# Reordering the seven block products of a channel mixer, and making their normed operand one tile earlier

## The chip, the cores and the metric

The kernel runs on one core of a Trainium2 chip. The metric is the device time of one execution in microseconds (us), as the median of several runs; less is better. All times of single instructions come from one profiled execution.

## The reference

A trunk of two layers over 512 frames of width 1024. Layer 0 mixes time with an RWKV-7 recurrence, layer 1 with chunked attention; both add attention into 256 memory tokens and an output projection. Each layer ends with the channel mixer that the change touches, a gated unit with a convolution over time:

```python
def conv_glu(h, w_in, conv_w, conv_b, w_out):
    seq = h.shape[1]
    gate, val = jnp.split(h @ w_in, 2, axis=-1)
    gp = jnp.pad(gate, ((0, 0), (CONV_W - 1, 0), (0, 0)))
    conv = conv_b + sum(conv_w[j] * gp[:, j:j + seq] for j in range(CONV_W))
    return (jax.nn.gelu(conv, approximate=False) * val) @ w_out
...
        x = x + conv_glu(rms_norm(x, ln2[layer]), ffn_in[layer], ffn_conv[layer],
                         ffn_conv_b[layer], ffn_out[layer])
```

D_FF is 2816, which is 22 tiles of 128 hidden columns; `w_in` makes a gate and a value for each.

## The kernel before

Activations lie transposed: 128 features on the partitions, 512 frames along a row. Every float32 operand is split into a high part and a low remainder, and a product is three passes of TensorE: high weight by high input, high weight by low input (these two alternate), then low weight by high input. The high part is made by ScalarE (`whi`, L169), the remainder by VectorE (`wlo`, L175). The split weights live in rings of three buffers each, the raw weights of the tiles below in a ring of two (`raw`).

A channel mixer (`ffn`) goes over the 22 hidden tiles in order, in two ways:

- `plain(j)`: tiles 0 to 5, 9, 13, 17, 20 and 21. Gate and value are 24 matmuls of 512 columns each (L198, L199, L202). Tiles 0 to 5 read the input before normalisation and multiply by `rho` afterwards (L390, L393).
- `seven(j)`: the other eleven tiles. Gate and value, each 2 by 2 blocks of inputs and frames, are made from seven block products instead of eight, Strassen-like. Each product (`prod`) is 12 matmuls of 256 columns: 8 with the high weights (L403), 4 with the low (L405). VectorE adds the weights up first (L415, L416, L419), and combines the results (L427, L429, L431, L433, L437).

The results lie in four PSUM tiles of 512 columns, one bank each, `f1` to `f4`; the ring `F` (name `psf`) has four banks. `h1` and `h2` are the halves of a bank. The products read pieces of the normed input (`XN`, tiles N) and four combinations of it (`XT`, tiles M). The framework that places the waits treats a bank as one thing: a product that starts a new sum in a bank waits until what was read from that bank, in either half, has been read.

The normed input and its combinations are made by `normed(k4)`, in four parts, each beside one plain tile. It uses a buffer of the ring `raw`, so the first weights for `seven` can be loaded only when these buffers come free.

The queues of the engines are filled by a list scheduler of the framework, which keeps to the order of the code unless it expects an engine to wait. So the order on an engine can differ from the order of the code; it is fixed when the program is built.

In layer 0 the matmul inputs of the seven products are called `r2h`/`r2l` (N) and `r1h`/`r1l` (M), in layer 1 `nh`/`nl` and `r2h`/`r2l`.

Of the kernel before, what the change touches and what calls it, by code (L numbers as in the profile page):

```python
# [13 lines left out]
ALU = mybir.AluOpType  # L14
# [5 lines left out]
S = 512  # L20
# [91 lines left out]
def trunk_kernel(ctx, tc, A, out):  # L112
    nc = tc.nc
    PE, V, SC, GP = nc.tensor, nc.vector, nc.scalar, nc.gpsimd
# [23 lines left out]
    def Vc(name, i):  # L138
        return vec[:, VOFF[name][0] + i:VOFF[name][0] + i + 1]
# [20 lines left out]
    def tmp(dt=F32, shape=(P, S)):  # L160
        return banks["tmp"].tile(list(shape), dt, name="tmp", tag="tmp")
# [180 lines left out]
    T1, T3, T2, T4 = range(4)  # L342

    def normed(k4, l, hp, xT, Nh, Nl, Mh, Ml):

        x2 = [tmp() for _ in range(2)]
        for u in range(2):
            k = k4 + 4 * u
            V.scalar_tensor_tensor(x2[u][:], xT[:, k], Vc(f"ln2_{l}", k), rho[:], op0=ALU.mult, op1=ALU.mult)
            split_to(Nh[:, k], Nl[:, k], x2[u][:])  # L350
        q = lambda i: x2[i // 2][:, i % 2 * 256:i % 2 * 256 + 256]
        su = hp.tile([P, 7, S], F32, name="raw", tag="raw", bufs=2)[:].rearrange("p a s -> p (a s)")[:, 0:1024]
        s_ = [su[:, i * 256:(i + 1) * 256] for i in range(4)]
        V.tensor_tensor(s_[T1], q(1), q(0), op=ALU.subtract)
        V.tensor_tensor(s_[T3], q(1), q(3), op=ALU.subtract)
        V.tensor_tensor(s_[T2], q(3), s_[T1], op=ALU.subtract)
        V.tensor_tensor(s_[T4], q(2), s_[T2], op=ALU.subtract)
        split_to(*(t[:, 2 * k4:2 * k4 + 2].rearrange("p a s -> p (a s)") for t in (Mh, Ml)), su)

    def ffn(l, hp, U, M, N, new_u, xT, after, last=None):  # L360


        (Uh, Ul), (Mh, Ml), (Nh, Nl) = U, M, N
        sp = hp.tile([P, 7, S], F32, name="sp", tag="sp")
        hid32 = {j: sp[:, j] for j in range(6)}

        def conv(g, j):
            c = tmp()
            SC.activation(c[:], g, AF.Identity, scale=Vc(f"cw2_{l}", j), bias=Vc(f"cb_{l}", j))
            conv_rest(c, g, j)  # L370
            return c

        def conv_rest(c, g, j):
            V.scalar_tensor_tensor(c[:, 1:S], g[:, 0:S - 1], Vc(f"cw1_{l}", j), c[:, 1:S], op0=ALU.mult, op1=ALU.add)
            V.scalar_tensor_tensor(c[:, 2:S], g[:, 0:S - 2], Vc(f"cw0_{l}", j), c[:, 2:S], op0=ALU.mult, op1=ALU.add)
            SC.activation(c[:], c[:], AF.Gelu)

        def plain(j, act, normed_):
            wg = load_w(A["ffn_in"][l, j, 0])
            wv = load_w(A["ffn_in"][l, j, 1])  # L380
            pg = ps_f()
            run(dense(pg[:], [(wg, K8)], act))
            pv = ps_f()
            run(dense(pv[:], [(wv, K8)], act))
            if normed_:
                c = conv(pg[:], j)
                V.tensor_tensor(hid32[j], pv[:], c[:], op=ALU.mult)
                return
            g = tmp()
            V.tensor_tensor(g[:], pg[:], rho[:], op=ALU.mult)  # L390
            c = conv(g[:], j)
            v = tmp()
            V.tensor_tensor(v[:], pv[:], rho[:], op=ALU.mult)  # L393
            V.tensor_tensor(hid32[j], v[:], c[:], op=ALU.mult)

        XN = lambda k0, h: [tuple(t[:, k0 + k, h * 256:h * 256 + 256] for t in (Nh, Nl)) for k in range(4)]
        XT = lambda i: [tuple(t[:, 2 * k + i // 2, i % 2 * 256:i % 2 * 256 + 256] for t in (Mh, Ml)) for k in range(4)]

        def prod(ps, w, x):
            (wh, wl), o = w  # L400
            for k in range(4):
                for n in range(2):
                    PE.matmul(ps, wh[:, o + k * P:o + k * P + P], x[k][n], start=k == n == 0, stop=False)  # L403
            for k in range(4):
                PE.matmul(ps, wl[:, o + k * P:o + k * P + P], x[k][0], start=False, stop=k == 3)  # L405

        def seven(j):

            raw = hp.tile([P, 7, S], F32, name="raw", tag="raw", bufs=2)
            g_, v_ = A["ffn_in"][l, j, 0], A["ffn_in"][l, j, 1]  # L410
            G1, S2, V2, G2, S3, S1, V1 = range(7)
            S4 = V1
            for o, src in ((V1, v_[:, 0:S]), (G1, g_[:, 0:S]), (V2, v_[:, S:2 * S]), (G2, g_[:, S:2 * S])):
                nc.sync.dma_start(raw[:, o], src)
            V.tensor_tensor(raw[:, S3:S1 + 1], raw[:, G1:V2 + 1:2], raw[:, V1:V1 + 1].to_broadcast([P, 2, S]), op=ALU.add)  # L415
            V.tensor_tensor(raw[:, S2], raw[:, S1], raw[:, G1], op=ALU.add)  # L416
            two = lambda o: split_w(raw[:, o:o + 2].rearrange("p a s -> p (a s)"), 1024)
            w_g1s2, w_s3s1, w_v2g2 = two(G1), two(S3), two(V2)
            V.tensor_tensor(raw[:, S4], raw[:, S2], raw[:, G2], op=ALU.add)  # L419
            w_s4 = split_w(raw[:, S4], S)  # L420
            h1, h2 = slice(0, 256), slice(256, 512)
            f1, f2, f3, f4 = (ps_f() for _ in range(4))
            g, c, v = tmp(), tmp(), tmp()
            prod(f1[:, h1], (w_g1s2, 0), XN(0, 0))
            SC.copy(g[:, h1], f1[:, h1])
            prod(f1[:, h2], (w_g1s2, S), XT(T2))
            V.tensor_tensor(g[:, h2], g[:, h1], f1[:, h2], op=ALU.subtract)  # L427
            prod(f2[:, h1], (w_s3s1, 0), XT(T3))
            V.tensor_tensor(c[:, h1], f2[:, h1], g[:, h2], op=ALU.subtract)  # L429
            prod(f3[:, h2], (w_s3s1, S), XT(T1))  # L430
            V.tensor_tensor(g[:, h2], g[:, h2], f3[:, h2], op=ALU.subtract)  # L431
            prod(f3[:, h1], (w_v2g2, 0), XT(T4))
            V.tensor_tensor(v[:].rearrange("p (a s) -> p a s", a=2), c[:, h1].unsqueeze(1).to_broadcast([P, 2, 256]),  # L433
                            f3[:].rearrange("p (a s) -> p a s", a=2), op=ALU.add)
            prod(f4[:, h1], (w_v2g2, S), XN(4, 0))
            prod(f4[:, h2], (w_s4, 0), XN(4, 1))
            V.tensor_tensor(g[:], g[:], f4[:], op=ALU.add)  # L437
            SC.activation(c[:], g[:], AF.Identity, scale=Vc(f"cw2_{l}", j), bias=Vc(f"cb_{l}", j))
            conv_rest(c, g[:], j)
            V.tensor_tensor(hid32[j], v[:], c[:], op=ALU.mult)  # L440

        hid = {}

        def halves(j, h, lo):
            hid[j] = h, lo
            split_to(h, lo, hid32[j])

        for j in range(PLAIN_RAW):
            plain(j, pair_of(Uh, Ul), False)
            if 1 <= j <= 4:  # L450
                normed(j - 1, l, hp, xT, Nh, Nl, Mh, Ml)
        u32 = [new_u(i, F32) for i in range(2)]
        for j in range(6, NFF):
            hid32[j] = u32[(j - 6) // 8][:, (j - 6) % 8]
        for j in range(PLAIN_RAW, NFF):
            if j in BY_SEVEN:
                seven(j)
            else:
                plain(j, pair_of(Nh, Nl), True)
            if j == NFF - 2:  # L460
                hl = [hp.tile([P, 7, S], F32R, name="hl", tag="raw", bufs=2) for _ in range(2)]
                for k in range(8, 15):
                    halves(k, hl[0][:, k - 8], hl[1][:, k - 8])
        for k in range(8):
            halves(k, Mh[:, k], Ml[:, k])
        uh = new_u(0, F32R)
        sl = hp.tile([P, 7, S], F32R, name="sl", tag="sp")
        for k in range(15, NFF):
            halves(k, uh[:, k - 15], sl[:, k - 15])
        for m in range(KD):  # L470
            us = []
            for lo, n in ((8, 7), (0, 8), (15, 7)):
                us.append((load_w(A["ffn_out"][l, m][:, lo * P:(lo + n) * P], n * P), list(range(lo, lo + n))))
            if m == KD - 1 and last is not None:
                last(us, lambda k: hid[k])
                break
            ps = ps_d()
            run(dense(ps[:], us, lambda k: hid[k]))
            V.tensor_tensor(xT[:, m], xT[:, m], ps[:], op=ALU.add)  # L479
            after(m)  # L480
# [612 lines left out]
    xT = mid.tile([P, KD, S], F32, name="xT")  # L1093
# [8 lines left out]
    hp = fctx.enter_context(tc.tile_pool(name="hpA", bufs=1))  # L1102
# [201 lines left out]
    with ExitStack() as fctx:  # L1304
        open_banks(fctx, S=2, F=4)
        open_tmp(fctx, 6)
        hp = fctx.enter_context(tc.tile_pool(name="hpB", bufs=1))
# [125 lines left out]
```

## Time and profile before

| | |
|---|---|
| median of 3 runs | 1368.42 us (1364.19 to 1369.57) |
| the profiled execution's own time | 1365.64 us |
| its span, first to last instruction | 1363.8 us |
| TensorE busy | 97% |
| VectorE busy | 68% |
| ScalarE busy | 49% |
| mean granted TensorE clock | 0.989 |

The profiled execution was 2.78 us faster than the median of the runs, so a sum made on it is carried to the median by that offset. A span is what one execution's records cover; the execution's own time adds 1.84 us around it.

### The profile page before, as it was taken

Reading aid. Unit: us, or ns where it says so; the run is one execution under the profiler, and the core shown is the slowest. Engines: PE = TensorE matmul, PEld = TensorE weight load, DVE = VectorE, ACT = ScalarE, POOL = GpSimd, SP = SyncE. Lnnn points to the kernel's source line nnn. Section 1 sums busy time; section 2 is a strip of 40 time slices with the busy share of each in tenths; the row PEclk is TensorE's granted clock in tenths of the full one; section 3 lists DMA queues with packets and bytes.
Section 4 is the critical chain, followed back from the end, with each engine's and each line's share of the span. In section 5 each row is a group of like instructions: output and inputs, shape, how many; then the busy total and the mean of one; then the engine's idle time right before and its main releaser. Section 6 shows DMA issues by size and latency. Waiting matters only on the chain. (4 is left out here: it accounts for less than half of the span.)

```text
span 1363.8 us, 24368 instructions
## 1 busy us (share of the span) xinstructions
PE 1318.7 (97%) x9826; PEld 1104.1 (81%) x9826; DVE 926.9 (68%) x1806; ACT 674.5 (49%) x1142; POOL 34.2 (3%) x57
## 2 busy tenths in 40 slices
PE   6999999999999999999999999999999999999996
PEld 5786777777788899998888778786788999888886
DVE  7865677664667998889333666747669988893324
ACT  6556566554544444455222576657444544472221
POOL 3000000000000000000000000000000000000000
PEclk9998999998999999999999999999999999999998
DMA  5376544551132332313323422222323332223322
GB/s 181 86 179 148 114 93 98 114 135 38 65 116 84 124 124 66 120 64 89 99 85 101 144 86 86 93 91 89 94 87 123 107 100 94 93 74 97 100 88 75
DMA packets 87904, 137.76 MB, mean 101 GB/s; under 512 B 44144, under 2 KB 47856, under 8 KB 87792
## 3 DMA queue, kind: packets, MB, share of 16 engines
q1 hardware_dynamic: 85056, 126.25, 30.9%
q0 software_dynamic: 2736, 9.96, 4.2%
q8 instruction: 77, 1.26, 0.4%
q14 instruction: 35, 0.29, 0.1%
HBM read 129.37 MB, written 6.82 MB: 100 GB/s over the span
## 5 line engine op out<-in xcount | busy, mean ns | idle before, releaser
L175 DVE TENSOR_TENSOR wlo<-wraw,whi 128x1024 fp32r<-128x1024 f32 (+1 forms) x139 | 165.3, 1191 | 140.7 <-PE psd L202 130.9
L169 ACT CAST whi<-wraw 128x1024 fp32r<-128x1024 f32 (+1 forms) x158 | 162.0, 1027 | 195.4 <-DMA wraw<-in_ffn_out_dram 50.1
L198 PE MATMUL psd<-r1h,whi 128*128 128x512 f32 (+1 forms) x399 | 161.0, 405 | 1.1 <-ACT whi L169 1.0
L199 PE MATMUL psd<-r1l,whi 128*128 128x512 f32 x336 | 132.9, 396 | 0.0
L169 ACT CAST whi<-raw 128x1024 fp32r<-128x1024 f32 x88 | 81.8, 940 | 85.2 <-PE psf L403 55.9
L202 PE MATMUL psd<-r1h,wlo 128*128 128x512 f32 (+1 forms) x399 | 107.0, 397 | 0.0
L175 DVE TENSOR_TENSOR wlo<-raw,whi 128x1024 fp32r<-128x1024 f32 x88 | 95.3, 1086 | 5.4 <-ACT whi L169 5.3
L198 PEld LDWEIGHTS psd<-r1h,whi 128*128 128x128 f32 x399 | 75.8, 190 | 20.6 <-issue 3.0
L202 PEld LDWEIGHTS psd<-r1h,wlo 128*128 128x128 f32 x399 | 72.9, 191 | 14.2 <-issue 0.3
L403 PE MATMUL psf<-r2h,whi 128*128 128x256 f32 x308 | 79.4, 288 | 1.8 <-ACT whi L169 1.3
L403 PE MATMUL psf<-r2l,whi 128*128 128x256 f32 x308 | 77.6, 283 | 0.0
L198 PE MATMUL psd<-r2h,whi 128*128 128x512 f32 (+1 forms) x200 | 77.4, 391 | 0.1
L199 PE MATMUL psd<-r2l,whi 128*128 128x512 f32 (+1 forms) x200 | 76.2, 384 | 0.8 <-DVE r2l L215 0.8
L199 PEld LDWEIGHTS psd<-r1l,whi 128*128 128x128 f32 x336 | 63.9, 190 | 11.1
L231 ACT ACTIVATE tmp<-xT 128x512 f32<-128x512 f32 x27 | 17.0, 631 | 103.4 <-DVE xT L479 88.4
L403 PEld LDWEIGHTS psf<-r2h,whi 128*128 128x128 f32 x308 | 58.8, 191 | 5.2 <-ACT whi L169 1.7
L403 PEld LDWEIGHTS psf<-r2l,whi 128*128 128x128 f32 x308 | 58.9, 191 | 0.2
L202 PE MATMUL psd<-r2h,wlo 128*128 128x512 f32 (+1 forms) x200 | 50.9, 386 | 0.0
L405 PE MATMUL psf<-r2h,wlo 128*128 128x256 f32 x308 | 49.4, 283 | 0.4 <-DVE wlo L175 0.4
L403 PE MATMUL psf<-r1h,whi 128*128 128x256 f32 x176 | 46.3, 294 | 0.4 <-DVE tmp L431 0.4
L198 PE MATMUL psd<-hl,whi 128*128 128x512 f32 (+1 forms) x119 | 44.4, 377 | 0.0
L199 PE MATMUL psd<-sl,whi 128*128 128x512 f32 (+1 forms) x119 | 44.4, 377 | 0.0
(450 smaller groups left out, 3270.9 us busy)
## 6 DMA issues: line engine op xcount, KB each, us to landing
wraw<-in_ffn_in_dram SPq DMA_DIRECT2D x44, 512.0 KB, 3.8
raw<-in_ffn_in_dram SPq DMA_DIRECT2D x88, 256.0 KB, 3.7
wraw<-in_ffn_out_dram SPq DMA_DIRECT2D x32, 448.0 KB, 3.4
wraw<-in_wA_dram SPq DMA_DIRECT2D x20, 512.0 KB, 4.2
wlo<-in_wA_dram POOLq DMA_DIRECT2D x17, 512.0 KB, 7.2
wraw<-in_w_out_dram SPq DMA_DIRECT2D x16, 512.0 KB, 3.8
wraw<-in_ffn_out_dram SPq DMA_DIRECT2D x16, 512.0 KB, 3.5
wraw<-in_wB_dram SPq DMA_DIRECT2D x8, 512.0 KB, 3.6
```

Of the source, the lines that this page charges most:

```text
L169: SC.copy(hi[:, :n], raw)
L175: V.tensor_tensor(lo[:, :n], raw, hi[:, :n], op=ALU.subtract)
L198: PE.matmul(ps, wh[:, j * P:(j + 1) * P], ah, start=start and n == 0, stop=False)
L199: PE.matmul(ps, wh[:, j * P:(j + 1) * P], al, start=False, stop=False)
L202: PE.matmul(ps, wl[:, j * P:(j + 1) * P], act(k)[0], start=False, stop=stop and n == len(ks) - 1)
L231: SC.activation(sq[:], src, AF.Square)
L403: PE.matmul(ps, wh[:, o + k * P:o + k * P + P], x[k][n], start=k == n == 0, stop=False)
L405: PE.matmul(ps, wl[:, o + k * P:o + k * P + P], x[k][0], start=False, stop=k == 3)
```

## The change

Two edits in `ffn`, for both layers. In `seven`, the second product goes into a new bank (`f2`) and not into the other half of the bank that ScalarE reads at that moment; the third goes back to the first bank; and the fifth is issued directly after the fourth, into the other half of the same bank, ahead of the VectorE instruction that reads the fourth's result. In the loop over tiles 0 to 5, `normed` is called beside tiles 0 to 3 and not 1 to 4. The arithmetic is the same, and no instruction is added or removed.

```diff
             prod(f1[:, h1], (w_g1s2, 0), XN(0, 0))
             SC.copy(g[:, h1], f1[:, h1])
-            prod(f1[:, h2], (w_g1s2, S), XT(T2))
-            V.tensor_tensor(g[:, h2], g[:, h1], f1[:, h2], op=ALU.subtract)
-            prod(f2[:, h1], (w_s3s1, 0), XT(T3))
-            V.tensor_tensor(c[:, h1], f2[:, h1], g[:, h2], op=ALU.subtract)
+            prod(f2[:, h1], (w_g1s2, S), XT(T2))
+            V.tensor_tensor(g[:, h2], g[:, h1], f2[:, h1], op=ALU.subtract)
+            prod(f1[:, h2], (w_s3s1, 0), XT(T3))
+            V.tensor_tensor(c[:, h1], f1[:, h2], g[:, h2], op=ALU.subtract)
+
             prod(f3[:, h2], (w_s3s1, S), XT(T1))
+            prod(f3[:, h1], (w_v2g2, 0), XT(T4))
             V.tensor_tensor(g[:, h2], g[:, h2], f3[:, h2], op=ALU.subtract)
-            prod(f3[:, h1], (w_v2g2, 0), XT(T4))
...
         for j in range(PLAIN_RAW):
             plain(j, pair_of(Uh, Ul), False)
-            if 1 <= j <= 4:
-                normed(j - 1, l, hp, xT, Nh, Nl, Mh, Ml)
+            if j < 4:
+                normed(j, l, hp, xT, Nh, Nl, Mh, Ml)
```

The lines after the reordered products stand one lower in the changed file: L431 is L433 there, and L433 is L434.

What becomes of it on the engines, at three places. First TensorE, tile 10 of layer 0 (the tile whose span the prediction follows matmul by matmul). `psf_6158` to `psf_6161` are its banks `f1` to `f4`; `whi_6141` holds the weights of the first pair of products, `whi_6145` of the second. Before, from the end of the first product to the start of the second in `f1`:

```order
L405 MATMUL psf_6158<-r2h_4908,wlo_6142 128x256 x4
L403 MATMUL psf_6159<-r1h_68,whi_6145 128x256
L403 MATMUL psf_6159<-r1l_69,whi_6145 128x256
...
L403 MATMUL psf_6158<-r1h_68,whi_6141 128x256
L403 MATMUL psf_6158<-r1l_69,whi_6141 128x256
```

and now:

```order
L405 MATMUL psf_6158<-r2h_4908,wlo_6142 128x256 x4
L403 MATMUL psf_6159<-r1h_68,whi_6141 128x256
L403 MATMUL psf_6159<-r1l_69,whi_6141 128x256
...
L405 MATMUL psf_6159<-r1h_68,wlo_6142 128x256 x4
L403 MATMUL psf_6158<-r1h_68,whi_6145 128x256
L403 MATMUL psf_6158<-r1l_69,whi_6145 128x256
```

Before, the scheduler put four matmuls of the product into `f2` between the first product and the second in `f1`; now the whole product into `f2`, twelve matmuls, stands there, and no product is cut in two any more. The same holds at `f3`: before, five matmuls of the sixth product stood between the fourth and the fifth; now the fifth follows the fourth with nothing between them.

Second VectorE in the same tile. `wlo_6155` is the last weight remainder of this tile, `wlo_6268` and `wlo_6272` are the first of the next. Before:

```order
L427 TENSOR_TENSOR tmp_6162<-tmp_6162,psf_6158 128x256
L175 TENSOR_TENSOR wlo_6155<-raw_6134,whi_6154 128x512
L429 TENSOR_TENSOR tmp_6163<-psf_6159,tmp_6162 128x256
L431 TENSOR_TENSOR tmp_6162<-tmp_6162,psf_6160 128x256
L175 TENSOR_TENSOR wlo_6268<-raw_6260,whi_6267 128x1024
L433 TENSOR_TENSOR tmp_6164<-tmp_6163,psf_6160 128x512
L415 TENSOR_TENSOR raw_6386<-raw_6386 128x1024
L175 TENSOR_TENSOR wlo_6272<-raw_6260,whi_6271 128x1024
```

and now:

```order
L427 TENSOR_TENSOR tmp_6162<-tmp_6162,psf_6159 128x256
L175 TENSOR_TENSOR wlo_6155<-raw_6134,whi_6154 128x512
L429 TENSOR_TENSOR tmp_6163<-psf_6158,tmp_6162 128x256
L175 TENSOR_TENSOR wlo_6268<-raw_6260,whi_6267 128x1024
L433 TENSOR_TENSOR tmp_6162<-tmp_6162,psf_6160 128x256
L434 TENSOR_TENSOR tmp_6164<-tmp_6163,psf_6160 128x512
L415 TENSOR_TENSOR raw_6386<-raw_6386 128x1024
L175 TENSOR_TENSOR wlo_6272<-raw_6260,whi_6271 128x1024
```

The subtraction from the fourth product's result (L431, now L433) went behind a weight remainder of the next tile, and waits for two products in place of one; L415, which waits for a load of raw weights, still stands ahead of the next tile's second remainder.

Third VectorE in layer 0 at the change from plain tiles to `seven`. `raw_5688` belongs to tile 6, the first of that kind, `psf_5626` and `psf_5651` are the gate and value of plain tile 5. Before:

```order
L357 TENSOR_TENSOR raw_5607<-tmp_5600,raw_5607 128x256
L390 TENSOR_TENSOR tmp_5676<-psf_5626,rho_71 128x512
L215 TENSOR_TENSOR r1l_69<-raw_5607,r1h_68 128x1024
L374 SCALAR_TENSOR_TENSOR tmp_5678<-tmp_5676,vec_67,tmp_5678 128x511
L415 TENSOR_TENSOR raw_5688<-raw_5688 128x1024
L375 SCALAR_TENSOR_TENSOR tmp_5678<-tmp_5676,vec_67,tmp_5678 128x510
L416 TENSOR_TENSOR raw_5688<-raw_5688 128x512
L419 TENSOR_TENSOR raw_5688<-raw_5688 128x512
L393 TENSOR_TENSOR tmp_5683<-psf_5651,rho_71 128x512
L175 TENSOR_TENSOR wlo_5696<-raw_5688,whi_5695 128x1024
```

and now (`psf_5579` is the value of plain tile 4):

```order
L415 TENSOR_TENSOR raw_5688<-raw_5688 128x1024
L375 SCALAR_TENSOR_TENSOR tmp_5606<-tmp_5604,vec_67,tmp_5606 128x510
L393 TENSOR_TENSOR tmp_5611<-psf_5579,rho_71 128x512
L416 TENSOR_TENSOR raw_5688<-raw_5688 128x512
L394 TENSOR_TENSOR sp_5193<-tmp_5611,tmp_5606 128x512
L419 TENSOR_TENSOR raw_5688<-raw_5688 128x512
L175 TENSOR_TENSOR wlo_5696<-raw_5688,whi_5695 128x1024
L415 TENSOR_TENSOR raw_5814<-raw_5814 128x1024
L390 TENSOR_TENSOR tmp_5676<-psf_5626,rho_71 128x512
```

Tile 6's weights are added up ahead of the gate of plain tile 5, and not after it. On the load queue (SP), tile 6's four raw loads (L414) stand one place earlier, ahead of the two loads for plain tile 9. From plain tile 20 on, each engine's order is as before, and nothing moves outside the two mixers.

## The prediction

> **What bounds the kernel now.** I read the page first: the busy line and the chain that ended last.
>
> ```profile
> PE 1318.7 (97%) x9826; PEld 1104.1 (81%) x9826; DVE 926.9 (68%) x1806; ACT 674.5 (49%) x1142; POOL 34.2 (3%) x57
> PE 33%; DVE 4%; ACT 2%; issue 1%; DMA 0%; DVEq 0%; SPq 0%; ACTq 0%
> ```
>
> TensorE carries the span; what the change can win is time in which TensorE stands still. The busy time does not show all of it, because the records of waiting matmuls overlap. So I looked at the stretches of the change: plain tiles 0 to 5 of layer 0, then from the first block product to plain tile 20 in each layer (busy time in us per engine, then granted clock).
>
> ```profile
> 411.00:471.50 60.50, 60.50 (x270) 49.87 (x268) 51.02 (x76) 27.54 (x34) 0.00 (x0) 1.00 0.33 106
> 472.97:621.86 148.89, 148.06 (x1068) 138.79 (x1069) 128.87 (x178) 75.50 (x101) 0.00 (x0) 1.00 0.28 87
> 1059.08:1207.23 148.15, 147.38 (x1068) 138.69 (x1069) 129.07 (x179) 75.48 (x101) 0.00 (x0) 1.00 0.27 87
> ```
>
> The clock is full there, and VectorE is busy 128.87 of 148.89 us. The timeline of TensorE then gives the pace without stops: an undisturbed product, the two halves of a plain tile, and the ends of the stretches.
>
> ```profile
> 520.14 0.28 PE L403 MATMUL psf<-r1h,whi 128*128 128x256 f32 x1
> 521.58 0.28 PE L403 MATMUL psf<-r2h,whi 128*128 128x256 f32 x1
> ...
> 627.33 0.39 PE L198 MATMUL psf<-r2h,whi 128*128 128x512 f32 x1
> 632.77 0.39 PE L198 MATMUL psf<-r2h,whi 128*128 128x512 f32 x1
> ```
>
> A product is 1.44 us (12 steps of 0.12), seven are 10.08. Half a plain tile is 5.44 (24 steps of 0.2267), a tile 10.88. The stretch holds eleven tiles of the one kind and three of the other: 11 × 10.08 + 3 × 10.88 = 143.52 us. It takes 148.89 and 148.15, so stops cost 5.37 in layer 0 and 4.63 in layer 1.
>
> Where they stand, in tile 10:
>
> ```profile
> 517.02 0.28 PE L403 MATMUL psf<-r1h,whi 128*128 128x256 f32 x1
> ...
> 517.38 0.28 PE L403 MATMUL psf<-r1l,whi 128*128 128x256 f32 x1
> 517.65 0.38 PE L403 MATMUL psf<-r1h,whi 128*128 128x256 f32 x1
> 517.87 0.28 PE L403 MATMUL psf<-r1l,whi 128*128 128x256 f32 x1
> ...
> 522.06 0.28 PE L403 MATMUL psf<-r2h,whi 128*128 128x256 f32 x1
> 522.25 0.39 PE L403 MATMUL psf<-r1h,whi 128*128 128x256 f32 x1
> 522.48 0.28 PE L403 MATMUL psf<-r1l,whi 128*128 128x256 f32 x1
> ```
>
> ```profile
> 517.22 0.37 ACT L425 COPY tmp<-psf 128x256 f32<-128x256 f32 x1 [1.55 <-PE psf L405]
> 521.78 0.42 DVE L431 TENSOR_TENSOR tmp<-tmp,psf 128x256 f32<-128x256 f32 x1 [0.97 <-PE psf L405]
> ```
>
> At 517.65 the product into the other half of `f1` starts 0.27 after the step before it instead of 0.12, and the next comes 0.22 later: 0.15 + 0.10 = 0.25 lost. It starts just as the copy of the first half ends (517.59). At 522.25 the same with L431, which ends at 522.20: 0.07 + 0.11 = 0.18. So 0.43 a tile, 4.7 for eleven; the rest is longer stops of the same kind and one of another, below. The view of waits counts them without the refill:
>
> ```profile
> PEld psf L403 <- ACT tmp L425: 3.4, 18, 0.2
> PEld psf L403 <- DVE tmp L431: 2.8, 6, 0.6
> DVE raw L415 <- DMA raw<-in_ffn_in_dram: 10.7, 10, 1.8
> ```
>
> The last place is where plain tile 5 ends and tile 6 begins:
>
> ```profile
> 469.69 1.98 PE L202 MATMUL psf<-uh,wlo 128*128 128x512 f32 x8
> 472.97 0.39 PE L403 MATMUL psf<-r2h,whi 128*128 128x256 f32 x1 [1.30 <-ACT whi L169]
> ...
> 1056.04 1.98 PE L202 MATMUL psf<-r1h,wlo 128*128 128x512 f32 x8
> 1059.08 0.36 PE L403 MATMUL psf<-nh,whi 128*128 128x256 f32 x1 [1.07 <-issue]
> ```
>
> The eight last matmuls take 8 × 0.2267 = 1.81 us, so the next could start at 471.50 and 1057.85. It starts 1.47 and 1.23 later: 2.70 in both layers.
>
> **The change part by part.** All stops together: 5.37 + 4.63 + 2.70 = 12.70 us. No instruction is added or removed, so the change can win these and give back what new waits cost.
>
> *First product, then `f2`.* At tile 10 the matmul that waits for the copy starts at 517.65, 0.63 us after the slot that follows the first product (517.02). Now the whole second product, 1.44, stands in between before `f1` is written again. 0.8 us is left over and the stop goes: 0.25 a tile. The second product's own bank is a fresh one of the ring; what was read from it belongs to a tile before.
>
> The Trainium skill, "PSUM — Partial Sum Buffer", section Terms, says that TensorE may not write a bank while ScalarE or VectorE reads it in the same quadrant, which speaks against returning to `f1` so soon. The trace agrees in that the start at 517.65 waits for a copy of the other half. By that rule a third product that comes before the copy's end pays 0.25 again, 22 × 0.25 = 5.5 us over the kernel; by the rows the copy is over by then.
>
> *Fifth product directly behind the fourth.* Nothing reads `f3` between them, so the stop goes: 0.18 a tile, more where L431 is late. VectorE's subtraction now waits one product longer, with L434, which waits for the fifth anyway, directly behind it, and L415 and a remainder of the next tile behind that. That remainder is needed by the next tile's third product, two products (2.88 us) into that tile.
>
> *Where the cover is thinnest.* In the third tile of a group (8, 12, 16) ScalarE's copy stands behind the previous tile's L438, which waits for VectorE's L437, which waits its turn behind a remainder. Today one such chain can be seen at tile 7:
>
> ```profile
> 480.89 1.05 ACT L169 CAST whi<-raw 128x1024 fp32r<-128x1024 f32 x1 [3.29 <-DVE raw L416]
> 481.98 1.23 DVE L175 TENSOR_TENSOR wlo<-raw,whi 128x1024 fp32r<-128x1024 f32 x1 [0.31 <-ACT whi L169]
> 483.72 0.68 DVE L437 TENSOR_TENSOR tmp<-tmp,psf 128x512 f32<-128x512 f32 x1
> 484.43 0.82 ACT L438 ACTIVATE tmp<-tmp,vec 128x512 f32<-128x512 f32 x1
> 485.15 0.35 ACT L425 COPY tmp<-psf 128x256 f32<-128x256 f32 x1
> ```
>
> I chain these durations for the new order, counted from the first product of the third tile. The cast's buffer comes free with the high passes of the sixth product before, at -1.7 (two products of 1.44 back, plus 8 × 0.12, plus the 0.2 from the slot at 517.02 to the copy at 517.22). Cast to -0.65, remainder to 0.6, L437 to 1.3, L438 (0.72 to the next start) to 2.0, copy to 2.35. The third product starts at 2.88, so 0.5 is left. If VectorE lags more, a stop comes back; at today's 0.25 in all six such tiles that is 1.5 us. Neither end is excluded; with 0.5 of slack I stand nearer to nothing and take 0.5.
>
> The Trainium skill, "TensorE: Matmul & The Clock Gate", Architectural detail, says that ScalarE's and VectorE's queues are strictly first in, first out. The row at 485.15, a copy that starts as L438 hands over, agrees. By that rule the copy cannot pass L438, and these six tiles could return up to 1.5; the sum would be 11.2 instead of 12.7.
>
> *A stop of another kind.* In tile 8:
>
> ```profile
> 493.63 1.23 DVE L415 TENSOR_TENSOR raw<-raw 128x1024 f32<-128x1024 f32 x1 [0.98 <-DMA raw<-in_ffn_in_dram]
> 495.97 1.22 DVE L175 TENSOR_TENSOR wlo<-raw,whi 128x1024 fp32r<-128x1024 f32 x1
> 497.24 0.74 PE L405 MATMUL psf<-r2h,wlo 128*128 128x256 f32 x4 [0.40 <-DVE wlo L175]
> ```
>
> L415 for tile 10, which is not urgent, waits for its load, and tile 8's first remainder is queued behind it. In the new order this L415 stands behind tile 8's first three remainders, so I count this stop (about half a microsecond in each layer) as gone. It is part of the 12.70.
>
> *`normed` one tile earlier.* It adds nothing, but its VectorE steps now fall on plain tile 0 instead of 4. One step of a part:
>
> ```profile
> 428.79 0.74 DVE L349 SCALAR_TENSOR_TENSOR tmp<-xT,vec,rho 128x512 f32<-128x512 f32 x1
> ```
>
> Two of L349, two remainders of half that width (0.69, by L390's row below), four steps of 256 columns (0.42, as L431) and one remainder of 1024 columns (1.23, as L175 above): 1.5 + 1.4 + 1.7 + 1.2 = 5.8 us. VectorE's idle time at tile 0:
>
> ```profile
> 414.14 0.75 DVE L374 SCALAR_TENSOR_TENSOR tmp<-tmp,vec 128x511 f32<-128x511 f32 x1 [0.89 <-ACT tmp L369]
> 417.31 0.69 DVE L393 TENSOR_TENSOR tmp<-psf,rho 128x512 f32<-128x512 f32 x1 [1.63 <-PE psf L202]
> 422.74 0.69 DVE L390 TENSOR_TENSOR tmp<-psf,rho 128x512 f32<-128x512 f32 x1 [3.01 <-PE psf L202]
> ```
>
> 0.89 + 1.63 + 3.01 = 5.5 us to 422.7; the 0.3 that does not fit is spread over the next tile, as it is today one tile later. Cost nothing, unless it delays tile 1's reads (a rival). At the other end, tile 6's L415 and L416 now stand ahead of plain 5's L390:
>
> ```profile
> 466.26 0.69 DVE L390 TENSOR_TENSOR tmp<-psf,rho 128x512 f32<-128x512 f32 x1 [0.15 <-PE psf L202]
> 470.83 0.68 DVE L416 TENSOR_TENSOR raw<-raw 128x512 f32<-128x512 f32 x1
> 471.87 2.95 ACT L169 CAST whi<-raw 128x1024 fp32r<-128x1024 f32 x3 [0.23 <-PE psf L202]
> ```
>
> Today L416 ends at 471.51 and the casts follow. With L416 before 466.3 and a cast of 1.05, the weights are ready some 4 us before 471.50, and the 2.70 goes. The four raw loads pass two loads for plain tile 9 on SP's queue, whose weights are used only after three tiles of seven products (30 us); I price that at nothing.
>
> *Sum.* -12.70 + 0.50 = -12.20. The profiled execution took 1365.64, so 1353.4; the median of the runs lies 2.78 above it, so 1356.2 us. That is 0.9% less; about 0.5% (6.8 us) is what a measurement of this kernel can tell from no change, the runs before lying within 5.4 us.
>
> **The rivals.**
>
> *B: the stop at the copy comes back at the third product in every tile.* It would if VectorE fell behind by more than 0.5 us in all of them, not just in the third ones. For it: VectorE's work stays 128.87 us while the stretch shrinks to 143.52, so its share rises from 87% to 90%. Against: the copy of the first and second tiles stands ahead of L438 or right after a waiting ScalarE, as at 517.22 (1.55 idle ahead of it). Price 22 × 0.25 = 5.5: 1365.64 - 12.70 + 5.5 + 2.78 = 1361.2.
>
> *C: the change moves its cost to plain tile 0.* If `normed` there is not hidden, L390 and L393 of tile 1 come late, their banks are not free and TensorE stops. Worst case all 5.8 us in both layers, 11.6: 1365.64 - 12.70 + 11.6 + 2.78 = 1367.3, no change. For it: the idle time fits by a hair. Against: the same part stands beside tiles 1 to 4 today and the window of these tiles has TensorE busy 60.50 of 60.50.
>
> *D: slower, by VectorE waiting in line for raw weights.* L415 waits for its load with remainders and L434 behind it; a faster TensorE asks for loads sooner, and the load can be issued only when VectorE has made the tile's last remainder. A layer leaves VectorE 143.5 - 128.9 = 14.6 us of idle time, 1.3 per tile of eleven. Loads that are later than that set TensorE's pace. The gain is gone at (12.7 + 29.2) / 22 = 1.9 us per tile, and it is 0.5% slower at 2.2. At 2.5 us: 22 × 2.5 - 29.2 = 25.8, giving 1365.64 - 12.70 + 25.8 + 2.78 = 1381.5. For it: the longest such wait is 1.8. Against: they number 10 in 22 tiles and sum to 10.7, 0.5 per tile, and in the new order L415 of the tile after a group stands later in the queue.
>
> **How the numbers follow.** My forecast 0.68, B 0.13, C 0.12, D 0.07. The forecast alone spans 1352.9 (no residual, no offset) to 1357.2 (residual 1.5, with the offset). To leave out no more than 2 in 10 the range must take in B: 1352.5 to 1362.5. B lies on the bound of 0.5%, so I split it: faster 0.68 + 0.07 = 0.75, same 0.06 + 0.12 = 0.18, slower 0.07.
>
> **What would show it.** Right: the stretch from the first product to plain tile 20 takes 143.5 to 145 us in both layers, no row of TensorE waiting for L425 in the waits or only in tiles 8, 12 and 16, none for L433; the matmul after plain tile 5 starts within 0.3 us of its slot; TensorE stays fully busy over plain tiles 0 to 5. B would show as 18 or more waits for L425, C as TensorE waiting for L390 or L393 near 420, D as TensorE waiting for `wlo` with L415 waiting over 1.9 us ahead of it. What would make it wrong most easily is that VectorE's order, which changed in many places, holds a remainder that TensorE needs.

## The result and the profile after

The changed kernel takes 1353.53 us (median of 4 runs, 1350.81 to 1356.04), the kernel before 1367.24 beside it: a ratio of 0.9901 with a 95% interval of 0.9872 to 0.9929. Timed once more beside the experiments it took 1351.70 against 1365.58, a ratio of 0.9898 (0.9883 to 0.9913). That is 13.7 and 13.9 us less, with intervals that begin at 9.7 and 11.9.

The page of the changed kernel, busy line and chain:

```profile
PE 1311.3 (97%) x9826; PEld 1104.0 (82%) x9826; DVE 923.9 (68%) x1806; ACT 675.2 (50%) x1142; POOL 34.1 (3%) x57
PE 34%; DVE 3%; ACT 2%; issue 1%; DMA 0%; DVEq 0%; SPq 0%; ACTq 0%
```

The shares look as before. The gain has to be read from the stretches: from the first block product to plain tile 20, layer 0 and layer 1, first in the profile that came with the result, then in a second profile of the same kernel.

```profile
472.94:617.97 145.03, 143.93 (x1069) 137.99 (x1068) 124.59 (x175) 73.47 (x99) 0.00 (x0) 1.00 0.28 90
1053.41:1197.65 144.24, 143.94 (x1069) 137.98 (x1068) 124.45 (x175) 73.59 (x99) 0.00 (x0) 1.00 0.28 91
```

```profile
471.44:615.02 143.58, 143.58 (x1070) 137.89 (x1068) 124.72 (x175) 73.78 (x99) 0.00 (x0) 1.00 0.29 91
1050.61:1194.18 143.57, 143.57 (x1069) 137.89 (x1068) 124.64 (x175) 73.69 (x99) 0.00 (x0) 1.00 0.29 91
```

Against the 143.52 us of a stretch without stops, the first profile has 1.51 and 0.72 us left, the second 0.06 and 0.05. Before, it was 5.37 and 4.63. The prediction named 143.5 to 145 us for each layer; layer 0 of the first profile is 0.03 us beyond that. Next, TensorE's timeline at the change from plain tile 5 to tile 6, in the first profile:

```profile
471.13 1.98 PE L202 MATMUL psf<-uh,wlo 128*128 128x512 f32 x8
472.94 0.28 PE L403 MATMUL psf<-r2h,whi 128*128 128x256 f32 x1
...
1051.59 1.98 PE L202 MATMUL psf<-r1h,wlo 128*128 128x512 f32 x8
1053.41 0.28 PE L403 MATMUL psf<-nh,whi 128*128 128x256 f32 x1
```

1.81 us after the last eight matmuls begin, the first product begins: the late start of 1.47 and 1.23 is gone. And at tile 10, ScalarE's copy, then the starts of the second, third and fifth product:

```profile
517.07 0.37 ACT L425 COPY tmp<-psf 128x256 f32<-128x256 f32 x1 [1.66 <-PE psf L405]
```

```profile
516.87 0.28 PE L403 MATMUL psf<-r1h,whi 128*128 128x256 f32 x1
...
518.31 0.28 PE L403 MATMUL psf<-r1h,whi 128*128 128x256 f32 x1
...
521.19 0.28 PE L403 MATMUL psf<-r1h,whi 128*128 128x256 f32 x1
```

The copy ends at 517.44, and the third product, which writes into the same bank, starts at 518.31, 1.44 after the second and not late; 0.87 us is left between them, where the prediction had 0.8. Its first matmul takes 0.28, not the 0.38 of one that had to wait. The fifth starts at 521.19 = 518.31 + 2 × 1.44.

What the first profile has left stands in the waits:

```profile
PE psf L403 <- ACT tmp L425: 1.4, 2, 1.1
DVE raw L415 <- DMA raw<-in_ffn_in_dram: 6.2, 6, 2.2
```

Two waits for the copy, and none for the subtraction that was L431. Both are in tile 8, one in each layer: 1.27 us in layer 0 and 0.46 in layer 1, counted from the slot, and 0.10 more each for the step behind them. That last part is called the refill below: after a matmul that waited, the next comes 0.22 us later and not 0.12. The timeline of layer 0 shows where the longer one begins, on VectorE beside tile 6, and how it reaches TensorE in tile 8 (L438 and L439 are the former L437 and L438):

```profile
483.80 1.23 DVE L415 TENSOR_TENSOR raw<-raw 128x1024 f32<-128x1024 f32 x1 [2.15 <-DMA raw<-in_ffn_in_dram]
484.94 1.22 DVE L175 TENSOR_TENSOR wlo<-raw,whi 128x1024 fp32r<-128x1024 f32 x1
...
495.40 0.68 DVE L438 TENSOR_TENSOR tmp<-tmp,psf 128x512 f32<-128x512 f32 x1
```

```profile
496.12 0.81 ACT L439 ACTIVATE tmp<-tmp,vec 128x512 f32<-128x512 f32 x1 [2.21 <-DVE tmp L438]
496.83 0.35 ACT L425 COPY tmp<-psf 128x256 f32<-128x256 f32 x1
```

```profile
497.24 0.39 PE L403 MATMUL psf<-r1h,whi 128*128 128x256 f32 x1 [1.10 <-ACT tmp L425]
```

L415 of tile 8 waits 2.15 us for its raw weights. From 483.80 on VectorE has no idle time until after L438 of tile 7 (at 495.40), so that is late; ScalarE's L439 is behind it, tile 8's copy behind that, and the third product starts 1.27 us after its slot. In the second profile the same L415 waits less, and no stop follows:

```profile
480.76 1.23 DVE L415 TENSOR_TENSOR raw<-raw 128x1024 f32<-128x1024 f32 x1 [0.61 <-DMA raw<-in_ffn_in_dram]
```

### The profile page after: what moved, and what is told of

The parts are those of the page before. It is cut to its first block, busy times and chain, and to the rows that moved or that the text cites. A ratio compares the mean times of both kernels' runs of the same rounds, so it can differ in the third digit from the quotient of the medians.

```text
span 1354.3 us, 24400 instructions
## 1 busy us (share of the span) xinstructions
PE 1311.3 (97%) x9826; PEld 1104.0 (82%) x9826; DVE 923.9 (68%) x1806; ACT 675.2 (50%) x1142; POOL 34.1 (3%) x57
## 5 line engine op out<-in xcount | busy, mean ns | idle before, releaser
L376 ACT ACTIVATE tmp<-tmp 128x512 f32<-128x512 f32 x44 | 27.7, 629 | 33.6 <-DVE tmp L375 33.0
```

## The experiments

**The two edits apart.** First the new order of the products without the move of `normed` (the loop keeps `if 1 <= j <= 4: normed(j - 1, ...)`).

> Only the new order of the products; normed beside tiles 1 to 4 as before. Theory (the two edits win separate stops): the stretch from the first product to plain tile 20 takes about 145.0 us in layer 0 and 144.2 in layer 1 as with the whole change (1.5 and 0.7 over 143.52), while the late start of tile 6 stays at 1.47 and 1.23 us. Gain 12.7 - 2.7 - 2.2 = 7.8 us, ratio about 0.994. Rival (the edits need each other: with normed late VectorE enters tile 6 behind, and the copy of tiles 7 and 8 comes late): the stretch is over 146.5 us in each layer, the gain under 5 us, ratio above 0.996.

Ratio 0.9933 (0.9920 to 0.9946), about 9.1 us.

```profile
471.12:614.79 143.67, 143.67 (x1069) 137.99 (x1069) 128.78 (x179) 75.17 (x101) 0.00 (x0) 1.00 0.29 92
1051.75:1195.39 143.64, 143.64 (x1069) 137.96 (x1070) 128.83 (x180) 75.12 (x101) 0.00 (x0) 1.00 0.29 92
```

```profile
471.12 0.38 PE L403 MATMUL psf<-r2h,whi 128*128 128x256 f32 x1 [1.30 <-ACT whi L169]
```

The late start stays (1.47 and 1.24), and the stops of the stretches are nearly all gone: they shrink by 9.73 us, and 0.27 is left. That is better than the 2.2 expected. The stop in tile 8 is absent: L415 of tile 8 stands behind tile 7's L427 here, and the waits of L415 for loads are short (1.4 us in 4 waits over both layers).

Then `normed` one tile earlier, with the products as before.

> Only normed beside tiles 0 to 3; the products as before. Theory: the late start of tile 6 (1.47 and 1.23 us) goes to under 0.1, the stretch of the products stays at 148 to 149 us in both layers; gain 2.7 us, ratio 0.998. Rival 1 (normed is not hidden beside tile 0): TensorE waits for L390 or L393 in tiles 1 and 2, the gain is eaten, ratio 1.000 or above. Rival 2 (VectorE's lag in the first group came from the late start): the stops for a weight remainder in tile 8 (about 0.5 a layer) go too, the stretch falls by 0.5 to 1 us a layer, gain 3.7 to 4.7.

Ratio 1.0003 (0.9990 to 1.0016). That is the first rival's number, but not its place: TensorE waits for neither L390 nor L393 in tiles 1 and 2. The late start is gone, and the stretches grew from 148.89 and 148.15 us:

```profile
470.45:620.61 150.16, 148.75 (x1070) 138.68 (x1069) 124.85 (x174) 73.75 (x99) 0.00 (x0) 1.00 0.26 86
1056.42:1205.98 149.56, 148.34 (x1069) 138.59 (x1068) 124.85 (x174) 73.77 (x99) 0.00 (x0) 1.00 0.27 86
```

```profile
DVE raw L415 <- DMA raw<-in_ffn_in_dram: 17.2, 14, 2.1
PEld psf L403 <- DVE tmp L431: 5.9, 11, 0.9
```

1.27 + 1.41 = 2.68 us more, nearly the 2.70 won at the start. That the two sums agree so closely is chance: layer 0 won 1.47 and gave back 1.27, layer 1 won 1.23 and gave back 1.41. L415 waits 17.2 us for loads in place of 10.7, and TensorE waits for L431 eleven times in place of six. One of them, of 0.67 us in tile 7, comes behind an L415 that waited 1.34; between the two VectorE has no idle time:

```profile
480.87 1.23 DVE L415 TENSOR_TENSOR raw<-raw 128x1024 f32<-128x1024 f32 x1 [1.34 <-DMA raw<-in_ffn_in_dram]
```

```profile
490.28 0.39 PE L403 MATMUL psf<-r1h,whi 128*128 128x256 f32 x1 [0.67 <-DVE tmp L431]
```

So the move alone brings nothing that could be measured. VectorE's queue stands behind a load for longer, and the reads that TensorE stops for come later. The rows show this chain for tile 7; for the other stops it is inferred from the two sums of waits.

**The two edits of the products apart.** Only the banks of the second and third product:

```diff
-            prod(f1[:, h2], (w_g1s2, S), XT(T2))
+            prod(f2[:, h1], (w_g1s2, S), XT(T2))
...
-            prod(f2[:, h1], (w_s3s1, 0), XT(T3))
+            prod(f1[:, h2], (w_s3s1, 0), XT(T3))
```

> Only the second product into f2 and the third into f1; the fifth still behind the VectorE instruction in the code, normed as before. Theory (a stop costs gap plus refill, 0.25 us in each of 22 tiles): no wait for L425 is left but in third tiles, those for L431 stay; the two stretches together shrink by about 5.5 us, ratio about 0.996. Rival (VectorE is behind anyway, so the time saved is spent at the next read): the waits for L431 grow from 2.8 us to over 5, the stretches shrink by less than 3 us.

```profile
473.13:618.53 145.40, 145.07 (x1068) 138.49 (x1069) 129.97 (x179) 75.77 (x101) 0.00 (x0) 1.00 0.28 90
1055.16:1201.89 146.73, 145.77 (x1068) 138.54 (x1069) 130.03 (x180) 75.38 (x101) 0.00 (x0) 1.00 0.28 90
```

The stretches shrink by 3.49 and 1.42, together 4.91 us; ratio 0.9970 (0.9958 to 0.9981). The waits for L425 fall from 18 to 4. The two longest stops among them (0.38 and 0.46 us) are not in third tiles, where they were expected, but in the second ones of layer 1, tiles 11 and 15. Then only the fifth product ahead of the subtraction:

```diff
-            V.tensor_tensor(g[:, h2], g[:, h2], f3[:, h2], op=ALU.subtract)
             prod(f3[:, h1], (w_v2g2, 0), XT(T4))
+            V.tensor_tensor(g[:, h2], g[:, h2], f3[:, h2], op=ALU.subtract)
```

> Only the fifth product directly behind the fourth; banks of the second and third as before, normed as before. Theory: no wait for the subtraction L431 is left, the 18 or more waits for the copy L425 at 0.25 us stay; the two stretches together shrink by the rest of the 10.0 us, about 3.5 to 4.5, ratio about 0.997. Rival (the copy then comes later, since VectorE's steps that it stands behind are later): the waits for L425 grow above their 3.4 us by as much, the stretches shrink by less than 2 us.

```profile
469.26:615.50 146.24, 145.99 (x1069) 138.50 (x1069) 128.50 (x178) 75.15 (x101) 0.00 (x0) 1.00 0.28 90
1052.29:1198.56 146.27, 145.87 (x1068) 138.41 (x1069) 128.68 (x179) 75.09 (x101) 0.00 (x0) 1.00 0.28 89
```

2.65 and 1.88, together 4.53 us; ratio 0.9971 (0.9961 to 0.9982). No wait for the subtraction is left, the copy's stay (16). 4.91 + 4.53 = 9.44 beside the 9.73 of both: the two kinds of stops add up, as the theory had it.

**The whole change again, and what makes the stop in tile 8.**

> The whole change again, beside the next three kernels. The earlier runs: the new order of the products alone 0.9933, normed alone 1.0003. If the two edits only half add up, because the stretch of the products gives 1.96 of the 2.70 us at the start of tile 6 back (2.23 us of stops with the whole change, 0.27 with the products alone), the ratio is 0.9933 - 0.74/1365 = 0.993, within its interval of the products alone. If they add up, 0.991.

The ratio is 0.9898 (0.9883 to 0.9913), below the interval of the products alone (0.9920 to 0.9946): with the products in the new order, the move of `normed` does pay. How much is less sure. The ratios differ by 4.8 us; the profiles show about 2.0, from 2.98 us of late start and stops with the products alone to 1.0 on average with the whole change. The intervals leave room for either. The second profile, shown above, has no stop in tile 8. To see whether the place of L415 in VectorE's queue or TensorE's earlier start makes it, `normed` was put so that tile 6's L415 still comes early, but tile 8's late:

```diff
-            if j < 4:
-                normed(j, l, hp, xT, Nh, Nl, Mh, Ml)
+            for k4 in {1: [0], 2: [1, 2], 3: [3]}.get(j, ()):
+                normed(k4, l, hp, xT, Nh, Nl, Mh, Ml)
```

> As the whole change, but the four parts of normed stand beside tiles 1, 2, 2 and 3. In the order of VectorE tile 6's L415 then still comes ahead of plain tile 5's gate, while tile 8's L415 stands behind tile 7's L427 and not ahead of tile 7's second remainder. Theory (the place of tile 8's L415 in the queue, where it waits for its load, makes the stop in tile 8): late start of tile 6 under 0.4 us, stretches at 143.5 to 144.0 us in both layers, no wait for L425 in tile 8; 1.5 to 2.2 us less than the whole change. Rival (TensorE starts 1.4 us sooner and the loads cannot be sooner, wherever L415 stands): a stop of 0.5 to 1.4 us in tile 8 of each layer stays.

```profile
472.28:616.38 144.10, 143.93 (x1070) 138.00 (x1068) 129.72 (x182) 74.18 (x101) 0.00 (x0) 1.00 0.29 91
1052.49:1196.06 143.57, 143.57 (x1069) 137.88 (x1068) 128.97 (x181) 74.31 (x101) 0.00 (x0) 1.00 0.29 91
```

No stop stands in tile 8, and there is no late start. Layer 0 loses 0.43 us in tile 6's first product, where a remainder comes late. The gain of 1.5 to 2.2 us over the whole change did not show: the ratio of 0.9908 (0.9892 to 0.9925) can't be told from that of the whole change. The missing stop is what the theory expected, but since the whole change can also run without it, this does not settle the cause. The next run did more, by an outcome that was not expected. The raw weights of tiles 8 and 12 go to a spare place:

```diff
-            raw = hp.tile([P, 7, S], F32, name="raw", tag="raw", bufs=2)
+            raw = u32[1][:, 0:7] if j in (8, 12) else hp.tile([P, 7, S], F32, name="raw", tag="raw", bufs=2)
```

> As the whole change, but the raw weights of tiles 8 and 12 go to a spare place (the space of later results) and not to the ring of two, so their loads need not wait for tile 6's last remainder. Theory (the stop in tile 8 comes from L415 waiting 2.15 us for a load in line): L415 of tile 8 waits under 0.3 us, the stop for L425 in tile 8 goes, the stretches fall from 145.03 and 144.24 to under 144 us. Rival (VectorE has simply too much to do in the first group, the wait for the load only filled time): L415 does not wait, but L425 still stops TensorE in tile 8 by 0.5 us or more.

```profile
482.74 1.23 DVE L415 TENSOR_TENSOR raw<-raw 128x1024 f32<-128x1024 f32 x1 [1.37 <-DMA raw<-in_ffn_in_dram]
```

```profile
496.18 0.39 PE L403 MATMUL psf<-r1h,whi 128*128 128x256 f32 x1 [0.80 <-ACT tmp L425]
```

The stop in layer 0 stayed, 0.96 + 0.10, but not for the rival's reason. Tile 8's own L415 moved ahead (to 475.61) and still waited 0.81 us there, not under 0.3, without a stop. Every load took its turn one tile sooner, so at the old place in VectorE's queue now stands the L415 of tile 10, and it waits 1.37 us for its own load. The ratio is 0.9915 (0.9900 to 0.9930). Taken from the first product of the layer, that L415 starts at 482.74 - 472.19 = 10.55, and the stop is 0.96; in the first profile of the change 483.80 - 472.94 = 10.86, with 1.27. The difference is 9.59 both times. So a start up to 9.59 us costs nothing. VectorE is free at 10.86 - 2.15 = 8.71, which leaves a slack of 0.9 us. In layer 1 of the run with the spare place the L415 of tile 10 starts at 9.65, and 0.05 + 0.10 is lost, as the sum has it. The sum was then tried on two more profiles of the whole change:

> The whole change, one more profile. Theory: VectorE's L415 of tile 8 may start up to 9.59 us after the first product of the layer; what it starts later comes through at tile 8's third product, with 0.1 more for the refill (in the first profile 10.86 and 10.05 gave stops of 1.27 + 0.10 and 0.46 + 0.10, in the second 9.32 gave none). So in each layer the stop in tile 8 is the start of L415 less 9.59. Rival (the stop has a cause of its own in ScalarE's queue): the stop does not follow this sum within 0.1 us.

> As the look before it: in each layer the stop at tile 8's third product is the start of tile 8's L415 after the first product, less 9.59 us, plus 0.1, or nothing where L415 starts sooner.

In the first of these, layer 0:

```profile
481.95 1.23 DVE L415 TENSOR_TENSOR raw<-raw 128x1024 f32<-128x1024 f32 x1 [2.21 <-DMA raw<-in_ffn_in_dram]
```

```profile
495.40 0.39 PE L403 MATMUL psf<-r1h,whi 128*128 128x256 f32 x1 [1.16 <-ACT tmp L425]
```

In the second, layer 1:

```profile
1058.57 1.23 DVE L415 TENSOR_TENSOR raw<-raw 128x1024 f32<-128x1024 f32 x1 [0.88 <-DMA raw<-in_ffn_in_dram]
```

The first product stands at 471.04 in the first of these, so L415 starts at 10.91, and the sum gives 1.32 + 0.10 = 1.42; the group lost 1.41. In its layer 1 L415 starts at 8.63 and no stop follows. In the second (first products at 469.94 and 1048.99) it starts at 8.99, without a stop, and at 9.58, with a loss of 0.08: right on the edge, just the refill. So the cause of the stop is shown: an L415 at this place in the queue that waits for its load, by more than 0.9 us.

What differs between the first and the second profile is the landing of the load, not its issue. The four loads of tile 8 are issued at the same place, 4.19 us after the layer's first product in the first profile and 4.20 in the second:

```profile
477.13 1.94 SPq L414 DMA_DIRECT2D raw<-in_ffn_in_dram  x4
```

```profile
475.64 1.94 SPq L414 DMA_DIRECT2D raw<-in_ffn_in_dram  x4
```

The median time from issue to landing is 4.3 us in the first and 3.6 in the second. Why it varies is not shown by these runs.

**How much VectorE may lag.** L415 is written twice, then three times; the repeats give the same values.

> As the whole change, but L415 is issued twice in each of the 22 tiles; the second gives the same values again and only costs VectorE about 1.14 us. Theory D of the prediction (between the first tile of a group and the next plain tile VectorE has no idle time to give, and 0.5 us of slack at the third tile's copy): two to three times 1.14 us of lag come through in each group, stops of 2 to 3 us a group, 8 to 11 us a layer, time 16 to 22 us above the whole change, ratio 1.004 to 1.009. Rival (what counts is the idle time of the whole stretch, 14.6 us a layer, against 12.5 us more work): under 3 us a layer, ratio under 0.997.

```profile
468.08:612.80 144.72, 144.08 (x1069) 137.98 (x1068) 136.84 (x188) 73.52 (x100) 0.00 (x0) 1.00 0.29 90
1048.42:1192.07 143.65, 143.65 (x1070) 137.93 (x1068) 135.93 (x187) 72.81 (x99) 0.00 (x0) 1.00 0.28 90
```

VectorE goes from 124.7 to 136.8 us and TensorE keeps its pace: the stops are 1.20 and 0.13 us, nearly all in the first group, and the ratio is 0.9910 (0.9894 to 0.9925). The 8 to 11 us a layer that were expected from the thin slack did not come. The outcome is the rival's, which counted the idle time of the whole stretch.

> As the whole change, but L415 is issued three times in each of the 22 tiles (the repeats give the same values). VectorE was busy 124.7 us of the 143.6 us stretch with the whole change and 136.8 and 135.9 with L415 twice; a third adds another 12.2, so about 148.5. Theory (the idle time of the stretch as a whole is what counts): TensorE cannot keep 143.52; the stretch is at least 149 us in each layer, 5 to 9 us of stops a layer, ratio about 0.998 to 1.003. Rival (VectorE's order or its overlaps give way again, as they did for the second): stretches under 147 us.

```profile
467.61:623.02 155.41, 147.55 (x1069) 141.12 (x1068) 149.36 (x198) 73.41 (x100) 0.00 (x0) 0.98 0.26 84
1058.40:1213.78 155.38, 147.52 (x1069) 141.10 (x1068) 149.28 (x198) 73.40 (x100) 0.00 (x0) 0.98 0.26 85
```

The ratio is 1.0073 (1.0054 to 1.0091), and the stretches are 11.9 us over 143.52. Not all of that is stops. There are three stops in each layer, each at the first product of the third tile of a group, 2.78 us late; with their refill they make 8.6 us a layer, within the 5 to 9 expected:

```profile
PE psf L403 <- ACT whi L169: 15.7, 6, 2.6
```

The first of them ends at 490.54. The cast that it waits for stands in ScalarE's queue behind L441, and that waits for VectorE, which has no idle time from 480.99 until after L440:

```profile
488.74 0.81 ACT L441 ACTIVATE tmp<-tmp,vec 128x512 f32<-128x512 f32 x1 [5.67 <-DVE tmp L440]
```

So with 149.4 us of work VectorE sets the pace at these places. The other 3.2 us a layer are slower matmuls: behind two of the three stops the granted clock is halved for 3.41 us, and a step takes 0.21 us and not 0.12:

```profile
491.91:495.32 3.41, 3.41 (x18) 3.41 (x18) 2.51 (x4) 1.39 (x3) 0.00 (x0) 0.50 0.00 0
```

Why the clock fell behind two of the stops and not behind the third is not shown.

## Why the prediction was right

The time lies in the range, the direction and the mechanism were the forecast's, and the likeliest time, 1356.2 us, was 2.7 us too high.

*All stops together, 12.70 us.* Confirmed by its parts: the late start 2.70 gone in all four profiles of the whole change; 10.00 us of stops down to 0.11 in the best of them. The second and third product's banks were priced at 22 × 0.25 = 5.5 and brought 4.91 alone; the fifth product had the rest, and brought 4.53 alone.

*The residual of 0.5, bounds 0 to 1.5.* The four profiles left 2.23, 0.11, 1.53 and 0.19 us in both layers together, 1.0 on average. So the bounds were too narrow for two of the four, and the size of the stop was mis-stated: it was priced at 0.25 in each of the six third tiles, and nearly all of it came in tile 8, up to 1.42 at a time. Of the other third tiles only 12 in layer 0 and 16 in layer 1 lost anything to speak of, a refill of 0.10 each and in the first profile alone. What fills tile 8's stop is L415's wait for a load that lands now sooner, now later, which the prediction did not put into this sum. The chain that it summed for the third tile, with 0.5 us left, is the one by which the wait arrives; the measured slack is 0.9. The Trainium skill, "TensorE: Matmul & The Clock Gate", Architectural detail, has the queues of ScalarE and VectorE strictly first in, first out, and the trace agrees in both links: nothing passes the waiting L415 at 483.80, and the copy does not pass L439 at 496.12.

*`normed` costs nothing.* That holds beside the new product order. VectorE's work at plain tile 0 was hidden: in layer 0 TensorE is busy from 411.00 to the first product, and in layer 1 for 63.41 of the 63.41 us from 990.00.

```profile
411.00:472.94 61.94, 61.94 (x276) 51.20 (x275) 57.08 (x88) 31.88 (x38) 0.00 (x0) 1.00 0.36 111
```

What the prediction did not see is that the 2.70 depends on the other edit. With the old order of the products 2.68 of it is given back. The prediction treated the two edits as separate terms of one sum, and the sum came out because the new order stood beside the move.

*The stop for a remainder in tile 8* went as said.

*Rival B* (VectorE behind at the copy in every tile) and *C* (cost moved to tile 0) did not come. *Rival D* named the engine and the wait that the residual is made of, with its price far off from deciding: L415 waited 6.2 us in six waits, not the 1.9 us in each tile at which the gain would be gone. B and D both took VectorE's work in the stretch as unchanged at 128.87 us. It fell to 124.6, because tile 6's weights are now added up ahead of the first product, so there was some 38 us of idle time in both layers, not D's 29.2. The kernel with L415 three times seems to confirm D's budget: 2 × 1.14 = 2.28 us more per tile should give, by D's sum, 1365.64 - 12.70 + (22 × 2.28 - 29.2) + 2.78 = 1376.7, and it took 1374.54. That is luck: L415 did not wait for its loads in that run's stretches, TensorE waited for casts and not for remainders, and some 6 us of the loss go with the halved clock.

*The level.* The miss of 2.7 us is as large as the offset of 2.78 that was added. It came from three runs of the kernel before, with a median of 1368.42; a fourth made that 1367.24, and beside the later experiments the medians were 1364.72, 1365.58 and 1366.03, close to the 1365.64 of the profiled execution. Without the offset the sum gives 1353.4, and 1353.53 was measured. That this fits to 0.1 us is partly luck, since the runs of the changed kernel lie 5 us apart. The gain beside the same runs, 13.7 for the 12.2 forecast, has an interval that begins at 9.7, so no term of the sum can be blamed for the difference.

## What to carry to other kernels

Where a matmul stops because its bank is still being read, write into another bank for as long as the read takes and come back; count the refill of about 0.1 us beside each gap, since the waits do not show it. An instruction that waits for a load should not stand in the queue ahead of those that feed the next product: look for the place where it stands, since an edit elsewhere can move it. Do not add up edits that meet at the same engine: the move of `normed` won its 2.7 us at the start of tile 6 in both cases, of which about 2 were left beside the new order and nothing without it. And before a loss is called a stop, look at the granted clock of the stretch.

## What the runs showed that was not expected

VectorE could take 12 us more work per 144 us stretch, 95% busy, with at most 1.2 us of stops on TensorE, although only 0.9 us of slack stood at the critical copy. That the work went into idle places of its queue is inferred from this; it was not traced place by place. With about 13 us more the stretch grew by 11 to 12: 7.4 to 8.5 of that as stops, and 3.2 as matmuls at the halved clock that followed them.
